# Operand sums, attention order, weight casts and a statistic's ring moved in a transformer layer on one core

## The chip, the core and the metric

The kernel runs on one core of a Trainium2 chip. The core has five engines that run side by side, each with its own in-order list of instructions: TensorE (PE) multiplies matrices, VectorE (DVE), ScalarE (ACT) and GpSimd (POOL) work element by element, SyncE (SP) does nothing here but start transfers. Transfers between DRAM and the on-chip memory run on 16 DMA engines; the instruction that starts one stands in an engine's list like any other, and waits there until its destination is free and its source is written. The metric is the device time of one execution in microseconds; the median of several runs counts.

## The reference

One step of one layer of a decoder, on 2048 new prompt tokens and 32 sample tokens (8 sequences of 4), model width 1024, all in fp32:

```
h = rmsnorm(x, n1);  z = h @ w_in            # split: hq hf hi hg | sq sk sv | ga gb
y_a = (rmsnorm(hgrn(hq, hf, hi, state)) * silu(hg)) @ w_up_a     # recurrent branch, 4 heads of 128
y_b = sink_attention(rotary(sq), rotary(sk), sv, window 128) @ w_up_b   # 8 query heads, 2 key heads of 64
m = sigmoid(ga) * y_a + sigmoid(gb) * y_b
x = x + m @ w_o
x = x + square(relu(rmsnorm(x, n2) @ w_ff1)) @ w_ff2             # width 4096
y = rmsnorm(x, normf)
```

The sample tokens attend to a cache of 128 keys and values for each sequence and start from a given recurrent state. Besides y, the kernel returns the new keys, values and states.

## The kernel before, in words

**Arithmetic.** Each fp32 operand is split in two parts: ScalarE casts it to a high half (fp32r), VectorE subtracts to get the low half. A product is three matmuls: high by high, high by low, low by high. The helpers are `split_out` (L257-259) for a source elsewhere and `split_in` (L143) in place. Large products with a whole pair of blocks use one level of a Strassen scheme (seven products for eight): `strassen_T` (L375-397) runs over pairs of weight columns (`Wpair`, L272-310) and chunks of tokens (`Unit`); its operands are A11, A12, A22 and the sums S1 to S4. `Wpair.early` loads and casts the two weight blocks B11 and B21 with which a pair's first two products (the tiles fB and fC) begin; `early` runs for the first pairs before the main loop, `rest` and `late` make the others.

**Stages.** The tokens are cut into four blocks of 512 (the fourth also holds the 32 sample tokens), in two pairs. For each block follow the projections by parts of w_in (C_HI values of the recurrence, C_HQ, C_SQ queries, C_SQ + 512 keys and values, C_HF), the attention, the levels of the recurrence, gate B (loop L1269-1283, eight steps j), gate A (L1290-1306, eight steps) and the output projection with w_o (L1384-1405, eight columns in four pairs). Before the third block a Strassen stage, named z, computes HQ, GA and GB for the whole second pair (L824-880). Its operands come from hidden values kept in DRAM; in front of it stand the projections skv and sq for the third and fourth block, whose results go to DRAM (zqk) from staging tiles (L826-837). After the fourth block follow, for each pair, the two feed-forward stages f1 (`strassen_T` again) and f2.

**The operand sums.** The first pair's feed-forward needs S1 to S4 of its normalised values h2d, which lie in DRAM. For each of four row groups k, `fr_load(k)` (L898-903) takes three tiles of the ring t4 and issues four loads on SP; `fr_sums` (L905-907) does four additions on VectorE (L605-608) and issues four stores dS on POOL's queue (L610). The ring t4 has three tiles, so one set fills it, and the next load waits until the stores of the one before have landed. The attention takes its cache tiles (kc, vc and others) from the same ring. Loads (L583) and additions are pinned. Before the change, sets 0 and 1 are in the C_HI projection of the third block (`fr_hook`, L922-930), sets 2 and 3 in the C_SQ and keys-and-values projections of the fourth (`sq_fr`, L914-917).

**What sets the order.** The program is traced in the order in which it is written; a planner then orders each engine's instructions by priority and by its own estimate of when each is ready. `pin` (L139-140) holds an instruction behind the one traced just before it on the same engine. TensorE's order in the attention and the recurrence is written out by hand: a list at L1131 of turns (T_), scores (S_), probabilities (P_) and values (V_) for the four subtiles, with `fill` steps between them that are matmuls of the C_HF projection. Small jobs are hung into loops: `late_at` (L559-568) calls the next of a list (for each block: the statistic `n2.stat`, its spreading `n2.spread` over the partitions, and `h2_out`, which scales and stores the normalised values) at given places of a projection; the list `todo` gives one job to each of the eight columns of the output projection (L1322-1383). In the third block the jobs are `reload` of the next block's operand on SP and `recast`, its split, both pinned; in the fourth they are loads and casts of the feed-forward's operands. In the fourth block's C_HI the sample tokens' scores, transposes (`smp_turn`) and values are hung in by `smp_at` (L1040). PSUM tiles come from four rings, mm, tp, hg and sw; the statistic of the last block (L1412) uses hg, as do the fC tiles of the feed-forward.

Weight tiles come from a ring of 12; a unit takes three (as loaded, high half, low half).

Of the kernel before, what the change touches and what calls it, by code (L numbers as in the profile page):

```python
# [16 lines left out]
P = 128  # L17
# [4 lines left out]
NKV = 2  # L22
# [21 lines left out]
def tile_hybrid_step(  # L44
# [225 lines left out]
    class Wpair:  # L270
# [2 lines left out]
        def __init__(u, N, n, src, wt):  # L273
            u.N, u.n, u.src, u.wt, u.ops = f"{N}_{n}", n, src, wt, {}

        def done(u, name, raw):
            v = (u.wt if name in ("T3", "T4") else wtile)(F32R, f"w1{name}_{u.N}").rearrange("p (s k c) -> p s k c", s=2, k=4)
            split_out(v[:, 0], v[:, 1], raw)
            u.ops[name] = v

        def early(u):
            v = wtile(F32, f"w1r0_{u.N}").rearrange("p (s k c) -> p s k c", s=2, k=4)
            for kh in range(2):
                nc.sync.dma_start(v[:, kh], u.src(u.n, kh)[:, 0:P].rearrange("(k p) c -> p k c", p=P))
                u.done(f"B{kh + 1}1", v[:, kh])

        def rest(u):
            b = []
# [86 lines left out]
    def strassen_T(N, npairs, src, chunks, A, st, fin, ahead, early, mid, free, wt):  # L375
        ws = [Wpair(N, n, src, wt) for n in range(npairs)]
        nch = len(chunks)
        units = [Unit(i, ws[i // nch], *chunks[i % nch], A, st, fin) for i in range(npairs * nch)]
        if free:
            units[-1].free, units[-1].ring = True, mm_ps  # L380
        for i in range(ahead):
            if i % nch == 0:
                units[i].pair.early()
            units[i].a(i < 4)
            early(i, units[i])
        for i, u in enumerate(units):
# [49 lines left out]
    def kmaj(x, r0, nk, c0, n):  # L436
        return x[r0 * P:(r0 + nk) * P, c0:c0 + n].rearrange("(k p) t -> p k t", p=P)
# [144 lines left out]
        for x, (r0, c0) in zip(r, ((0, 0), (4, 0), (0, Th), (4, Th))):  # L582
            pin(nc.sync.dma_start(x, h2d[b][(r0 + k) * P:(r0 + k + 1) * P, c0:c0 + Th]))  # L583

    def ff_sums(b, v, r, k, loaded=False):
# [19 lines left out]
        pin(tt(s1, a21, a22, ALU.add), loaded)  # L605
        pin(tt(s2, s1, a11, ALU.subtract), loaded)
        pin(tt(a21, a11, a21, ALU.subtract), loaded)
        pin(tt(a12, a12, s2, ALU.subtract), loaded)
        for n, x in (("S2", s2), ("S1", s1), ("S3", a21), ("S4", a12)):
            nc.gpsimd.dma_start(sd[b][n][k * P:(k + 1) * P, :], x)  # L610

    def op_load(b, v, x, r0, c0, now=True):
        out = []
# [18 lines left out]
    for bi in range(nblk):  # L632
# [193 lines left out]
        if zs and not odd:  # L826
            stage = [wk.tile([P, 768], F32, tag="stg", bufs=4, name=f"stg{c}") for c in range(ncb)]

            def st_skv(ps, kind, c, nr):
                nc.scalar.copy(stage[c][:, 512:768], ps)  # L830

            def st_sq(ps, kind, c, nr):
                nc.scalar.activation(qk_out(stage[c][:, 0:512]), qk_in(ps), AF.Copy, scale=HD ** -0.5)
                nc.scalar.dma_start(zqk[sb][c * P:(c + 1) * P, :], stage[c])
# [70 lines left out]
        def fr_sums():  # L905
            k, r = fr.pop()
            ff_sums(0, None, r, k, True)

        if not zs:
            colN512(C_HI, f"hi{B}", ev_v, *((late_at(0, 2, 3), None) if bi else (first_stat, first_split)))  # L910
# [1 line left out]
                first = bi == 0 and h < 2  # L912
                colT(C_HQ, h, f"hq{B}{h}", ev_q, sw_ps if first else mm_ps, (lambda: spread(rb0, rs0[:, 0], bt, "first")) if first and h == 0 else None)
        if odd or not zs:  # L914
            sq_late = late_at(0, 2, 3)
            sq_fr = iter([lambda: fr_load(2), none, none, lambda: [fr_sums(), fr_load(3)], none, none, none, fr_sums, none] if zs else [none] * 9)
            colN512(C_SQ, f"sq{B}", ev_sq, lambda i, ul: [sq_late(), next(sq_fr)()])
            colN(C_SQ + 512, f"skv{B}", ev_skv, lambda: next(sq_fr)())
        else:
            for c in range(ncb):  # L920
                nc.gpsimd.dma_start(qkv[:, c, :], zqk[sb][c * P:(c + 1) * P, :])
            nc.gpsimd.dma_start(qW, kmaj(zd[sb], 0, HH, z0 + ns, bt))  # L922
            def fr_hook(i, ul):
                if i == 0:
                    fr_load(0)
                elif i == 2:
                    fr_sums()
                    fr_load(1)
                elif i == 3:
                    fr_sums()  # L930

            colN512(C_HI, f"hi{B}", ev_v, fr_hook)
# [104 lines left out]

        if zs and odd:
            nc.gpsimd.dma_start(qW, kmaj(zd[sb], 0, HH, z0 + ns, bt))
            smp_at = {0: lambda: [smp_scores(kv) for kv in range(NKV)], 1: lambda: [smp_turn(kv) for kv in range(NKV)], 2: smp_values} if smp else {}  # L1040
            colN512(C_HI, f"hi{B}", ev_v, lambda i, ul: smp_at[i]() if i in smp_at else None)

        kts = {-1: k_last}
# [84 lines left out]
                    n -= 1  # L1128

        T_, S_, P_, V_ = swa_turn, swa_scores, swa_probs, swa_values  # L1130
        for f, c in ((T_, 0), (fill, 6), (S_, 0), (T_, 1), (fill, 12), (S_, 1), (T_, 2), (fill, 30), (P_, 0), (fill, 10), (V_, 0), (S_, 2), (T_, 3), (fill, 10), (P_, 1),  # L1131
                     (fill, 10), (V_, 1), (S_, 3), (fill, 10), (P_, 2), (fill, 8), (V_, 2), (fill, 16), (P_, 3), (fill, 8), (V_, 3)):
            f(c * len(segs) if f is fill else c)
        fill(1000)
# [135 lines left out]
        for j in range(KD):  # L1270
            if j % 2 == 0:
                ub = unit(
                    [(kv * HD, (kv + 1) * HD, w_ub[kv * 256:(kv + 1) * 256, j * P:j * P + 256].rearrange("(k p) c -> p k c", p=HD)) for kv in range(NKV)],
                    4, f"ub{B}{j}")
            for _ in gate(C_GB, j, ub, b_acts, lambda j, t0, n: pb[:, j, t0:t0 + n], "b"):
                pass
            if zs and j < 4:
                nc.vector.tensor_copy(ga[:, 2 * j, 0:1], pb[:, j, 0:1])
                nc.gpsimd.dma_start(ga[:, 2 * j:2 * j + 2, :], kmaj(zd[sb], HH + KD + 2 * j, 2, z0, T))
            if sb == 0 and j % 2 == 1:  # L1280
                sum_next()
            elif sb == 0:
                side_next(bi)
# [7 lines left out]
        for j in range(KD):  # L1291
            if sb == 0 and j % 2 == 1:
                sum_next()
            elif sb == 0:
                side_next(bi)
            if j == 0 and zs:
                ua_next = unit_rows(w_ua, 0, 4, 0, 256, f"ua{B}0", True)
            if j % 2 == 0 and zs:
                ua = ua_next
                if j + 2 < KD:  # L1300
                    ua_next = unit_rows(w_ua, 0, 4, (j + 2) * P, 256, f"ua{B}{j + 2}", True)
            elif j % 2 == 0:
                ua = unit_rows(w_ua, 0, 4, j * P, 256, f"ua{B}{j}")
            for t0, n, o in gate(C_GA, j, ua, a_acts, lambda j, t0, n: ga[:, j, t0:t0 + n] if zs else t2(f"ta_{B}{j}_{t0}")[:, 0:n], "a"):
                (nc.vector if j >= KD - 2 else nc.gpsimd).tensor_tensor(o, o, pb[:, j, t0:t0 + n], ALU.add)
                split_out(mT[j // 4][:, 0, j % 4, t0:t0 + n], mT[j // 4][:, 1, j % 4, t0:t0 + n], o)

        while side.get(bi):
            side_next(bi)
# [38 lines left out]
        elif not odd:  # L1348
# [405 lines left out]
```

## Time and profile before

| | us |
|---|---|
| median of 3 runs | 2844.31 (2840.08 to 2846.9) |
| the profiled execution | 2856.07 |
| its span | 2854.1 |
| TensorE busy | 2743.9 (96%) |
| VectorE busy | 1788.6 (63%) |
| ScalarE busy | 1110.6 (39%) |
| GpSimd busy | 489.8 (17%) |

All durations in the text are from the profiled execution, whose mean granted TensorE clock was 0.987 of full speed. Its time has been read thus: an engine's busy time is the sum of its instructions; a wait is the time in which an engine stood before an instruction, put down to what ended it; the chain of waits is the way back from the last instruction through whatever released each step.

### The profile page before, as it was taken

The page shows a single profiled execution, that of the slowest core. Times are in us where ns is not written, and L with a number is a line of the kernel's source. Part 1 is how long each engine was busy: PE and PEld are TensorE (multiplying, and loading weights), DVE is VectorE, ACT ScalarE, POOL GpSimd, SP SyncE. Part 2 cuts the span into 40 slices and gives each one's busy share as a digit, 9 for nine tenths or more (in the row PEclk, how much of TensorE's full clock was granted, in tenths as well). Part 3 has the DMA queues.
Part 4 walks back from the last instruction along what each step waited for, and adds up shares of the span by engine and source line. Part 5 has one row for each costly group of instructions (what it writes and reads, how often), then busy time and mean ns, then how long its engine had stood idle before and what let it go on. Part 6 is the DMA issues. An engine that isn't in the chain of part 4 may idle for free.

```text
span 2854.1 us, 50092 instructions
## 1 busy us (share of the span) xinstructions
PE 2743.9 (96%) x20053; PEld 2414.4 (85%) x20053; DVE 1788.6 (63%) x2905; ACT 1110.6 (39%) x2070; POOL 489.8 (17%) x782
## 2 busy tenths in 40 slices
PE   8999999999899989989899999999998999999998
PEld 7778877788799967767898888887888999999997
DVE  5675646646764375535667777765567777664556
ACT  4542445323344353324325333434443233343332
POOL 1100211002200101320231222220002333320001
PEclk9999999999999999999999999999999999999999
DMA  5237662377733533651266444696566444485553
GB/s 187 76 107 236 206 190 67 105 235 264 231 122 113 158 91 106 211 169 51 87 196 208 161 162 159 228 320 230 195 195 205 157 144 152 146 288 187 188 187 114
DMA packets 344481, 487.60 MB, mean 171 GB/s; under 512 B 23432, under 2 KB 220824, under 8 KB 344248
## 3 DMA queue, kind: packets, MB, share of 16 engines
q1 hardware_dynamic: 289112, 329.10, 37.0%
q0 software_dynamic: 42880, 140.22, 13.6%
q10 hardware_dynamic: 12256, 15.08, 1.5%
q8 instruction: 157, 2.57, 0.4%
q14 instruction: 76, 0.62, 0.1%
HBM read 353.64 MB, written 130.68 MB: 170 GB/s over the span
## 4 chain that ended last, share of the span: by engine, by line
PE 76%; DMA 8%; DVE 5%; issue 5%; ACT 3%; POOL 2%; SPq 0%; POOLq 0%; ACTq 0%; DVEq 0%
PE f L1585 6%; PE f L1584 6%; PE f L1586 6%; PE fB_f L264 4%; PE fB_f L266 4%; PE fB_f L265 4%; PE fD_f L264 2%; PE fD_f L266 2%; PE fD_f L265 2%; PE wob L1394 1%; PE wob L1392 1%; PE wob L1393 1%; PE fB_z L264 1%; PE fB_z L266 1%; PE fB_z L265 1%
## 5 line engine op out<-in xcount | busy, mean ns | idle before, releaser
L1584 PE MATMUL f<-f2S,hw2T 128*128 128x264 f32 (+1 forms) x576 | 184.5, 320 | 2.5 <-ACT hw2T L151 2.5
L1586 PE MATMUL f<-f2S,lw2T 128*128 128x264 f32 (+1 forms) x576 | 184.2, 320 | 1.0 <-DVE lw2T L152 1.0
L1585 PE MATMUL f<-f2S,hw2T 128*128 128x264 f32 (+1 forms) x576 | 184.1, 320 | 0.0
L264 PE MATMUL fB_f<-S,w1T_f 128*128 128x264 f32 (+1 forms) x384 | 123.0, 321 | 3.1 <-ACT c_f L327 2.5
L1584 PE MATMUL f<-f2A,h_w2B 128*128 128x264 f32 (+1 forms) x384 | 122.4, 319 | 0.0
L1585 PE MATMUL f<-f2A,h_w2B 128*128 128x264 f32 (+1 forms) x384 | 122.3, 319 | 0.0
L1586 PE MATMUL f<-f2A,l_w2B 128*128 128x264 f32 (+1 forms) x384 | 122.3, 318 | 0.0
L265 PE MATMUL fB_f<-S,w1T_f 128*128 128x264 f32 (+1 forms) x384 | 122.2, 319 | 0.0
L266 PE MATMUL fB_f<-S,w1T_f 128*128 128x264 f32 (+1 forms) x384 | 121.9, 319 | 0.0
L152 DVE TENSOR_TENSOR lw2T<-lw2T,hw2T 128x1024 fp32r<-128x1024 f32 x64 | 78.2, 1224 | 65.9 <-ACT hw2T L151 65.0
L1584 PEld LDWEIGHTS f<-f2S,hw2T 128*128 128x128 f32 x576 | 108.7, 189 | 10.5 <-ACT hw2T L151 3.0
L151 ACT CAST hw2T<-lw2T 128x1024 fp32r<-128x1024 f32 x64 | 67.2, 1051 | 128.8 <-DMA lw2T<-w_T 128.8
L1586 PEld LDWEIGHTS f<-f2S,lw2T 128*128 128x128 f32 x576 | 108.4, 188 | 9.5 <-DVE lw2T L152 1.8
L1585 PEld LDWEIGHTS f<-f2S,hw2T 128*128 128x128 f32 x576 | 108.8, 189 | 7.5
L1394 PE MATMUL wob<-m_b,l_wob 128*128 128x512 f32 (+2 forms) x320 | 112.1, 350 | 2.8 <-DVE l_wob L258 2.8
L1392 PE MATMUL wob<-m_b,h_wob 128*128 128x512 f32 (+2 forms) x320 | 112.1, 350 | 0.0
L1393 PE MATMUL wob<-m_b,h_wob 128*128 128x512 f32 (+2 forms) x320 | 111.8, 349 | 0.0
L152 DVE TENSOR_TENSOR f2S<-f2S 128x1024 fp32r<-128x1024 f32 (+1 forms) x64 | 79.0, 1240 | 43.8 <-ACT f2S L151 43.2
L258 DVE TENSOR_TENSOR w1T_f<-w1r_f,w1T_f 128x512 fp32r<-128x512 f32 x128 | 87.4, 688 | 26.2 <-ACT w1T_f L257 25.9
L257 ACT CAST w1T_f<-w1r_f 128x512 fp32r<-128x512 f32 x128 | 77.1, 619 | 65.2 <-PE fB_f L266 27.9
L1511 POOL DMA_DIRECT2D u_A<-c_f x106 | 57.3, 541 | 239.2 <-DVE c_f L1495 230.9
L258 DVE TENSOR_TENSOR l_w2B<-rw2B,h_w2B 128x1024 fp32r<-128x1024 f32 x48 | 58.8, 1224 | 62.6 <-ACT h_w2B L257 52.7
(845 smaller groups left out, 9302.8 us busy)
## 6 DMA issues: line engine op xcount, KB each, us to landing
w1r_f<-w_ff SPq DMA_DIRECT2D x64, 512.0 KB
lw2T<-w_T SPq DMA_DIRECT2D x64, 512.0 KB
rw2B<-w_ff SPq DMA_DIRECT2D x48, 512.0 KB
f2S<-u_S SPq DMA_DIRECT2D x32, 528.0 KB
ws<-w_ff SPq DMA_DIRECT2D x32, 512.0 KB
r_wob<-w_o SPq DMA_DIRECT2D x32, 512.0 KB
f2S<-u_S SPq DMA_DIRECT2D x32, 512.0 KB
u_S<-s_f POOLq DMA_DIRECT2D x96, 132.0 KB, 2.3
```

The costliest lines, as they stand in the source:

```text
L152: pin(nc.vector.tensor_tensor(lo, F(lo), F(hi), ALU.subtract), on)
L257: pin(nc.scalar.copy(dh, src), on)
L258: pin(nc.vector.tensor_tensor(dl, src, F(dh), ALU.subtract), on)
L264: nc.tensor.matmul(ps, wh, ah, start=(first and k == 0), stop=False, skip_group_check=not first)
L265: nc.tensor.matmul(ps, wh, al, start=False, stop=False, skip_group_check=not first)
L266: nc.tensor.matmul(ps, wl, ah, start=False, stop=(last and k == 3), skip_group_check=not first)
L1392: nc.tensor.matmul(p, wh, ah, start=(k == 0), stop=False)
L1393: nc.tensor.matmul(p, wh, al, start=False, stop=False)
L1394: nc.tensor.matmul(p, wl, ah, start=False, stop=(k == KD - 1))
L1584: nc.tensor.matmul(ps, wh, ah, start=first, stop=False, skip_group_check=cont)
L1585: nc.tensor.matmul(ps, wh, al, start=False, stop=False, skip_group_check=cont)
L1586: nc.tensor.matmul(ps, wl, ah, start=False, stop=lastk, skip_group_check=cont)
```

## The change

1. `early` gets a flag that pins its casts and subtractions; `strassen_T` sets it for the first pair, in z and in both feed-forward stages:

```diff
-                units[i].pair.early()
+                units[i].pair.early(i == 0)
```

2. In front of z, the queries come before the keys and values. The store of zqk goes with the later one, and the second block's late jobs move:

```diff
-            colN(C_SQ + 512, f"skv{B}", st_skv, late_at(1))
-            colN512(C_SQ, f"sq{B}", st_sq, late_at(0, 1))
+            colN512(C_SQ, f"sq{B}", st_sq, late_at(0, 2))
+            colN(C_SQ + 512, f"skv{B}", st_skv, late_at(1))
```

3. The operand sums leave the projections of the third and fourth block. Sets 0 and 1 go into the third block's gates, sets 2 and 3 into its output projection, whose other jobs move by up to a column (`fr_sums` and `ff_sums` also get a queue as an argument, which stays POOL's everywhere):

```diff
+        fr_at = {("b", 0): lambda: fr_load(0), ("b", 5): fr_sums, ("b", 6): lambda: fr_load(1), ("a", 3): fr_sums} if zs and not odd else {}
...
-            todo += [lambda: [reload(0, 0), reload(0, 2)], none, lambda: recast(0, 0), lambda: [recast(0, 2), reload(1, 0)], lambda: reload(1, 2), lambda: recast(1, 0), lambda: recast(1, 2)]
+            todo += [lambda: [fr_load(2), reload(0, 0)], lambda: reload(0, 2), fr_sums, lambda: [fr_load(3), recast(0, 0)],
+                     lambda: [recast(0, 2), reload(1, 0)], lambda: [fr_sums(), reload(1, 2)], lambda: recast(1, 0), lambda: recast(1, 2)]
```

4. In the fourth block's C_HI the sample's transposes and values come one unit later:

```diff
-            smp_at = {0: lambda: [smp_scores(kv) for kv in range(NKV)], 1: lambda: [smp_turn(kv) for kv in range(NKV)], 2: smp_values} if smp else {}
+            smp_at = {0: lambda: [smp_scores(kv) for kv in range(NKV)], 2: lambda: [smp_turn(kv) for kv in range(NKV)], 3: smp_values} if smp else {}
```

5. In the attention of every block six matmuls of fill move from in front of P_0 to behind it:

```diff
-(T_, 2), (fill, 30), (P_, 0), (fill, 10), (V_, 0)
+(T_, 2), (fill, 24), (P_, 0), (fill, 16), (V_, 0)
```

6. The last block's statistic takes its PSUM tiles from another ring:

```diff
-            n2.ring = hg_ps
+            n2.ring = sw_ps
```

More of the change, by code (lines that the diff above doesn't have):

```diff
@@ L274, in __init__, with done, early @@
             u.N, u.n, u.src, u.wt, u.ops = f"{N}_{n}", n, src, wt, {}
-        def done(u, name, raw):
+        def done(u, name, raw, on=False):
             v = (u.wt if name in ("T3", "T4") else wtile)(F32R, f"w1{name}_{u.N}").rearrange("p (s k c) -> p s k c", s=2, k=4)
-            split_out(v[:, 0], v[:, 1], raw)
+            split_out(v[:, 0], v[:, 1], raw, on)
             u.ops[name] = v
-        def early(u):
+        def early(u, on=False):
             v = wtile(F32, f"w1r0_{u.N}").rearrange("p (s k c) -> p s k c", s=2, k=4)
@@ L284, in early @@
                 nc.sync.dma_start(v[:, kh], u.src(u.n, kh)[:, 0:P].rearrange("(k p) c -> p k c", p=P))
-                u.done(f"B{kh + 1}1", v[:, kh])
+                u.done(f"B{kh + 1}1", v[:, kh], on)
         def rest(u):
@@ L583, in ff_rows, with ff_sums @@
             pin(nc.sync.dma_start(x, h2d[b][(r0 + k) * P:(r0 + k + 1) * P, c0:c0 + Th]))
-    def ff_sums(b, v, r, k, loaded=False):
+    def ff_sums(b, v, r, k, loaded=False, q=nc.gpsimd):
         Th = Ths[b]
@@ L609, in ff_sums @@
         for n, x in (("S2", s2), ("S1", s1), ("S3", a21), ("S4", a12)):
-            nc.gpsimd.dma_start(sd[b][n][k * P:(k + 1) * P, :], x)
+            q.dma_start(sd[b][n][k * P:(k + 1) * P, :], x)
     def op_load(b, v, x, r0, c0, now=True):
@@ L830, in st_skv @@
                 nc.scalar.copy(stage[c][:, 512:768], ps)
+                nc.scalar.dma_start(zqk[sb][c * P:(c + 1) * P, :], stage[c])
             def st_sq(ps, kind, c, nr):
                 nc.scalar.activation(qk_out(stage[c][:, 0:512]), qk_in(ps), AF.Copy, scale=HD ** -0.5)
-                nc.scalar.dma_start(zqk[sb][c * P:(c + 1) * P, :], stage[c])
+            colN512(C_SQ, f"sq{B}", st_sq, late_at(0, 2))
             colN(C_SQ + 512, f"skv{B}", st_skv, late_at(1))
-            colN512(C_SQ, f"sq{B}", st_sq, late_at(0, 1))
             Th = Ths[sb]
@@ L903, in fr_load, with fr_sums @@
             ff_rows(0, fr[-1][1], k)
-        def fr_sums():
+        def fr_sums(q=nc.gpsimd):
             k, r = fr.pop()
-            ff_sums(0, None, r, k, True)
+            ff_sums(0, None, r, k, True, q)
+        fr_at = {("b", 0): lambda: fr_load(0), ("b", 5): fr_sums, ("b", 6): lambda: fr_load(1), ("a", 3): fr_sums} if zs and not odd else {}
         if not zs:
@@ L914, in tile_hybrid_step @@
         if odd or not zs:
[L915 to L918, printed above, removed]
+            colN512(C_SQ, f"sq{B}", ev_sq, late_at(0, 2, 3))
+            colN(C_SQ + 512, f"skv{B}", ev_skv)
         else:
@@ L922, in tile_hybrid_step @@
             nc.gpsimd.dma_start(qW, kmaj(zd[sb], 0, HH, z0 + ns, bt))
[L923 to L932, printed above, removed]
+            colN512(C_HI, f"hi{B}", ev_v)
         ob = op(6, F32R, "ob_" + B)[:, 0:8 * T].rearrange("p (s k t) -> p s k t", s=2, k=4)
@@ L1130, in tile_hybrid_step @@
         T_, S_, P_, V_ = swa_turn, swa_scores, swa_probs, swa_values
-        for f, c in ((T_, 0), (fill, 6), (S_, 0), (T_, 1), (fill, 12), (S_, 1), (T_, 2), (fill, 30), (P_, 0), (fill, 10), (V_, 0), (S_, 2), (T_, 3), (fill, 10), (P_, 1),
+        for f, c in ((T_, 0), (fill, 6), (S_, 0), (T_, 1), (fill, 12), (S_, 1), (T_, 2), (fill, 24), (P_, 0), (fill, 16), (V_, 0), (S_, 2), (T_, 3), (fill, 10), (P_, 1),
                      (fill, 10), (V_, 1), (S_, 3), (fill, 10), (P_, 2), (fill, 8), (V_, 2), (fill, 16), (P_, 3), (fill, 8), (V_, 3)):
@@ L1279, in tile_hybrid_step @@
                 nc.gpsimd.dma_start(ga[:, 2 * j:2 * j + 2, :], kmaj(zd[sb], HH + KD + 2 * j, 2, z0, T))
+            if ("b", j) in fr_at:
+                fr_at["b", j]()
             if sb == 0 and j % 2 == 1:
@@ L1306, in tile_hybrid_step @@
                 split_out(mT[j // 4][:, 0, j % 4, t0:t0 + n], mT[j // 4][:, 1, j % 4, t0:t0 + n], o)
+            if ("a", j) in fr_at:
+                fr_at["a", j]()
         while side.get(bi):
```

## The prediction

> **What bounds the kernel now.** I read the page first, then TensorE's waits, then the chain of waits at the longest of them, and last the timelines of the engines on which the change puts work.
>
> ```profile
> span 2854.1 us, 50092 instructions
> PE 2743.9 (96%) x20053; PEld 2414.4 (85%) x20053; DVE 1788.6 (63%) x2905; ACT 1110.6 (39%) x2070; POOL 489.8 (17%) x782
> ```
>
> TensorE is busy for 2743.9 of 2854.1 us, so it sets the time, and 110.2 us of idle time are all that a change of order can touch. The change takes no matmul away and adds none. So the working is a list of TensorE's waits: columns are the waiting tile and line, who released it, microseconds in total, times, longest.
>
> ```profile
> PE sp_b2c L1070 <- ACT kt_b2c L953: 9.2, 1, 9.2
> PE kcT L973 <- DMA kc<-cache_swa_k: 8.0, 1, 8.0
> PE fB_f L264 <- DVE y L1591: 4.6, 1, 4.6
> PE pTs L1019 <- DVE ss L1014: 4.0, 1, 4.0
> PE fB_z L264 <- ACT stg L833: 2.8, 1, 2.8
> PE fC_z L264 <- DVE p_z L342: 2.6, 1, 2.6
> PE n_fb L216 <- DVE p_f L342: 2.1, 1, 2.1
> PE po_b1c L1117 <- DVE sm_b1c L1090: 1.7, 1, 1.7
> PE po_b0c L1117 <- DVE pc_b0c L1108: 1.2, 1, 1.2
> ```
>
> The first, second and fourth rows are 21.2 us in the third and fourth block, and the change touches each. Now what stands behind the first, in rows of SP's timeline and of the chain of waits (start, duration, what):
>
> ```profile
> 988.28 1.85 SPq L583 DMA_DIRECT2D fr<-h2d  x4
> 990.23 1.08 SPq L138 DMA_DIRECT2D r_hfb<-w_in  x2
> 997.30 2.81 DMA dS<-fr
> 1000.26 1.80 SPq L583 DMA_DIRECT2D fr<-h2d  x4
> 1002.16 7.14 DMA r_hgb<-w_in
> 1009.37 1.04 ACT h_hgb L257
> 1012.10 3.62 PE sp_b2c L1070 x32
> 1019.20 1.99 PE sp_b2c L1070 x32
> ```
>
> SP's queue had issued a weight load by 991.31 and then stood until 1000.26 in front of the second set of fr loads, whose tiles come free only when the sums of the first set have landed in DRAM (997.30 + 2.81). The weight load r_hgb stood behind, ScalarE's cast h_hgb waited for that, and the casts of the attention's keys wait behind the cast. After the wait the first 32 score matmuls took 3.62 us, the next 32 only 1.99: TensorE's clock was low after idling.
>
> **The change part by part.** All is summed against the profiled execution (2856.07 us with its 2854.1 us span). It lies 11.8 us above the median of the runs, 2844.31, and I carry the difference over to the median unchanged.
>
> *The third block's attention start.* The fr loads and sums leave this block's C_HI, so r_hgb could go out at 991.3 instead of 1002.16, which is 10.9 us earlier and more than the wait of 9.2. With the wait go 3.62 - 1.99 = 1.6 us of slow matmuls. Next late are the keys' own casts on ScalarE; I leave 2 us for them: **-8.8** (bounds -5 and -10.8).
>
> *The fourth block's cache turn, and the sample's scores.*
>
> ```profile
> 1250.72 2.87 DMA dS<-fr
> 1253.71 4.15 DMA kc<-cache_swa_k
> 1259.93 0.43 PE ps_hib_-1_11965 L191
> 1268.77 9.69 DMA r_hfb<-w_in
> 1278.54 1.04 ACT h_hfb L257
> 1282.63 0.45 PE pTs L1019
> 1283.29 0.43 PE ps_hib_-1_11965 L191
> 1288.73 0.23 PE ps_hib L192
> ```
>
> kc lies in the same ring of three tiles as fr: its load starts at 1253.71, just after the last sums landed (1253.59). After the change the last sums belong to the third block's output projection, which ends before the fourth block begins, so the 8.0 us go, and about three matmuls at 0.43 instead of 0.23: **-8.6** (-6.5 and -8.7). The sample's transposes pTs waited 4.0 us for a softmax whose ScalarE steps stood behind the cast h_hfb (1278.54), which waited for its load. One place later they have one more unit of C_HI in front, 24 matmuls of 0.23, which is 5.5 us and more than 4.0. From 1283.29 to 1288.7 about twelve matmuls cost 0.43 instead of 0.23, another 2.4: together **-6** (-4 and -6.4).
>
> *The order of the attention.* V_0 gets 16 matmuls of fill in front instead of 10, P_0 gets 24 instead of 30. Six at 0.23 are 1.4 us, taken off the waits of po on the two rows shown: 1.4 of the 1.7 and all of the 1.2, and a little of smaller waits of the same kind. **-3** (-4 to +1, since P_0 now comes 1.4 us earlier and may wait for its softmax).
>
> *The statistic in the sw ring.* n_fb waited 2.1 us for DVE to read a feed-forward tile in the hg ring. In the sw ring, which the first feed-forward units don't use, that wait goes: **-2** (0 to -2.1).
>
> *The pinned casts.* This is the part with a price. A pinned cast stands behind whatever was traced before it on its engine, and at the start of the feed-forward that is the cast of S1.
>
> ```profile
> 1518.65 1.13 ACT L257 CAST w1B_f<-w1r_f 128x512 fp32r<-128x512 f32 x2
> 1534.82 0.69 DVE L258 TENSOR_TENSOR w1B_f<-w1r_f,w1B_f 128x512 fp32r<-128x512 f32 x1 [0.20 <-ACT w1B_f L257]
> 1535.51 0.40 PE L264 MATMUL fB_f<-A,w1B_f 128*128 128x512 f32 x1
> 1536.80 1.98 ACT L151 CAST S<-S 128x1024 fp32r<-128x1024 f32 x2
> 1537.86 2.36 DVE L152 TENSOR_TENSOR S<-S 128x1024 fp32r<-128x1024 f32 x2 [0.21 <-ACT S L151]
> ```
>
> Before, pair 0's weights were cast at 1518.65, and the first matmul ran at 1535.51. S1's casts end at 1538.78 and its subtractions at 1540.22. One weight cast (0.57) behind the former gives a first matmul at about 1539.4; the low half (0.69) gives the third at 1540.9 instead of 1536.0: 4.9 us, and 2.4 for the slow matmuls after such a pause (as at 1283.29), 7.3 in all. The other bound is 0: TensorE's order is not pinned here, the later pairs' weights are not pinned either, and two groups of 12 matmuls (5.5 us) of the next pair could fill the hole. No row decides between them; I take the middle, **+4** (0 to +7.3). [...]
>
> The same pin in the stage before the third block stands behind the casts of its operands, with the projections sq and skv exchanged and the late steps of the second block moved; the stores of zqk, as many as before, go out on ScalarE's queue with skv, now the later of the two. Its start waits 2.8 + 2.6 us now; the exchange can take that away (-5) or the pinned casts can add as much as at the feed-forward (+6): **0**. In the second feed-forward the start waits 4.6 us for y already, and two casts of 1.13 us together fit under that: **0** (up to +3).
>
> *The sums in their new places.* Each set is four DVE instructions and four issues on POOL.
>
> ```profile
> L605 DVE TENSOR_TENSOR fr<-fr x4: 685/692/695, 995.6 to 1249.0; 128x512 f32<-128x512 f32 x4
> L610 POOL DMA_DIRECT2D dS<-fr x16: 540/540/586, 996.6 to 1251.9; - x16
> 1156.20 1.22 DVE L258 TENSOR_TENSOR l_uab<-r_uab,h_uab 128x1024 fp32r<-128x1024 f32 x1
> PE yab L167 <- DVE l_uab L258: 0.8, 1, 0.8
> 1142.33 1.28 POOL L1305 TENSOR_TENSOR ga_b<-ga_b,pb_b 128x512 f32<-128x512 f32 x1 [1.07 <-DVE ga_b L1267]
> 1148.76 2.20 POOL L1305 TENSOR_TENSOR ga_b<-ga_b,pb_b 128x512 f32<-128x512 f32 x1 [2.06 <-DVE ga_b L1267]
> ```
>
> 4 x 0.69 = 2.8 us of DVE. In gate A's third step they are traced just ahead of l_uab, a pinned instruction for which TensorE already waits 0.8: nearly all of it shows, **+2.5** (0 to +6, the upper end if the waiting DMAs' issues, 4 x 0.54 = 2.2, hold up POOL's additions too). In gate B and in the output projection DVE has room between evictions; the only reader near is the low half of w_o: **+0.7** for the two sets there (0 to +3), 0 for the set in gate B. POOL's addition takes 1.28 us in one row and 2.20 in another of the same shape. [...]
>
> Sum: -8.8 - 8.6 - 6 - 3 - 2 + 4 + 0 + 2.5 + 0.7 = -21.2. That gives 2834.9 for an execution like the profiled one, and 2844.31 - 21.2 = **2823** for the median.
>
> **The rivals.**
>
> *Half the gain (0.15).* ScalarE works in order, and the casts of the keys and of the sample's softmax stand behind weight casts whichever load is late. If that keeps 4.8 us of the first wait and all 6 of the sample's, the sum is -10.4: 2834. For it: both waits end on ScalarE behind a cast. Against it: in both chains the load, not the cast, is the long piece (7.14 and 9.69 against 1.04).
>
> *More (0.13).* The hole at the feed-forward is filled by the next pair (-4), and the exchange of sq and skv clears the 5 us at the stage's start: -30, which is 2814.
>
> *No change (0.10).* The fr loads were not what held SP: r_hgb might have no free weight tile either until about 1002, and kc might be held by another tile of the ring. Then the first two terms (17.4) fall out and -3.8 is left: 2840.5, within 0.2% (5.7 us, about what a measurement of this kernel can tell from no change). Against it: the loads follow each other on SP without a pause at 1000.26 to 1002.16, and dS landed 0.1 us before kc started.
>
> *Slower (0.08).* The moved fr loads stay pinned on SP and wait in turn for the sums before them.
>
> ```profile
> 1169.76 0.97 SPq L138 DMA_DIRECT2D r_wob<-w_o  x2
> 1162.00:1206.00 44.00, 43.95 (x195) 36.06 (x194) 27.72 (x28) 19.76 (x24) 14.31 (x16) 1.00 0.57 186
> ```
>
> In gate B's seventh step and in steps 0 and 3 of the projection, weight loads stand behind them. Each could cost what it cost before, 9.2 + 1.6 = 10.8; three are 32.4, and the sum becomes +11: 2855. It decides where SP stands longer than the weights' lead. The projection takes 44 us for eight columns, so the weights of the third pair, issued at 1169.8, are wanted at 1162 + 22 = 1184: 14 us, of which 7 for landing and 2.3 for cast and subtraction are used. SP would have to stand over 5 us; it stood 9.0 in the third block's attention, but there the loads came right behind the sums. Here one or two steps lie between.
>
> **How the numbers follow.** My forecast has the chance 0.54; the likeliest time is 2823. Three cases are faster by over 0.2% (below 2838.6): 0.54 + 0.15 + 0.13 = 0.82. Within it lies no change, 0.10; above 2850.0 the last, 0.08. The range starts at 2812, which holds the better rival and little beyond it, and ends at 2840, which holds the half gain and leaves out most of the case of no change and the slower one: about 0.17 lie above and 0.03 below.
>
> **What would show it.** In the changed profile the waits of sp_b2c on kt_b2c, of kcT on kc and of pTs on ss should be gone or under 2 us, and the score matmuls of the third block should all take 2.0 per 32. fB_f should show a first wait of 4 to 5 us at the first feed-forward's start, or another pair's group in its place. l_uab in the third block should have TensorE waiting some 3 us. Wrong would be a wait of over 5 us on a weight cast in the third block's gates or projection, or a wait of over 8 us still at the attention's start.

## The result and the profile after

The changed kernel takes 2818.86 us (median, 2811.82 to 2820.34) where the kernel before takes 2842.20 on the same chip: a ratio of 0.9911 with a 95% interval of 0.9889 to 0.9933, so 23.3 us less, and clear of the 0.2% that can be told apart. The forecast was 21.2 us less, a median of 2823.

The profiled execution of the changed kernel took 2811.82 us and is the shortest of its runs; that of the kernel before (2856.07) lay above its median. The two profiles are thus 44 us apart, 21 more than the medians, and stages that the change doesn't touch differ by 2 us and more. So stages are compared here over all profiles, and a difference counts only where it stays whenever the part in question stays.

The first lines of the page after:

```profile
span 2810.0 us, 50089 instructions
PE 2730.1 (97%) x20053; PEld 2403.9 (86%) x20053; DVE 1791.2 (64%) x2905; ACT 1110.0 (40%) x2070; POOL 490.9 (17%) x782
```

The same number of matmuls, and 13.8 us less TensorE busy time: the mean granted clock rose from 0.987 to 0.993, so most of this should be matmuls that ran at a low clock before. A change of order thus touched more than the idle time of 110.2 us that the prediction began from. The waits of TensorE after, those that answer to the rows shown of before and those that are new (waiting tile and line, releaser, us in total, times, longest):

```profile
PE yab L167 <- DVE l_uab L258: 3.8, 1, 3.8
PE wob L1388 <- ACT h_wob L257: 3.2, 2, 1.7
PE n_fb L216 <- DVE carry L245: 2.0, 1, 2.0
PE fB_f L264 <- DVE y L1587: 1.7, 1, 1.7
PE ps_skvb L176 <- ACT stg L830: 1.5, 1, 1.5
PE fB_f L264 <- ACT w1B_f L257: 0.6, 1, 0.6
PE kcT L964 <- ACT SV_b L940: 0.3, 1, 0.3
PE po_b0c L1108 <- DVE pc_b0c L1099: 0.3, 1, 0.3
```

The 9.2 of the attention's start, the 8.0 of the cache, the 4.0 of the sample and the 2.1 of the statistic in its old form are gone; kcT waits 0.3. In their place stand 3.8 us in gate A, 3.2 on w_o's weights, and some 2.6 at the feed-forward's start.

The lengths of the stages, each from the first matmul of one tile to the first of the next, worked out from the starts in the traces (us):

| stage | before | after | sums_old | fill_old | turn_old | sq_old | no_pin | pin_z | ring_hg | sums_c |
|---|---|---|---|---|---|---|---|---|---|---|
| second block, attention | 42.2 | 38.8 | 38.8 | 42.2 | 38.8 | 38.8 | 38.8 | 38.8 | 38.8 | 38.8 |
| second block's output projection to the end of z | 295.2 | 288.7 | 289.0 | 288.3 | 288.4 | 292.5 | 294.6 | 290.6 | 289.4 | 288.8 |
| third block, attention to gate B | 98.4 | 85.9 | 99.2 | 91.1 | 82.7 | 85.6 | 86.7 | 87.9 | 86.2 | 83.9 |
| third block, gate A | 23.9 | 29.1 | 24.0 | 29.6 | 29.6 | 29.5 | 29.1 | 28.3 | 29.6 | 23.9 |
| third block, output projection | 43.9 | 50.2 | 43.8 | 49.5 | 49.6 | 50.4 | 50.3 | 49.6 | 49.4 | 46.3 |
| fourth block, queries | 28.7 | 30.4 | 28.7 | 29.8 | 30.5 | 29.6 | 30.1 | 29.8 | 29.8 | 28.7 |
| keys and values, cache turn | 24.4 | 15.9 | 23.9 | 15.9 | 15.9 | 15.9 | 15.9 | 15.9 | 15.9 | 15.9 |
| C_HI with the sample | 44.7 | 35.6 | 37.2 | 35.6 | 41.0 | 35.8 | 35.6 | 35.6 | 35.6 | 35.6 |
| last output projection to first fB_f | 48.4 | 52.2 | 52.2 | 52.2 | 52.2 | 52.2 | 48.4 | 48.4 | 48.4 | 48.4 |

From before to after the rows change by -3.4, -6.5, -12.5, +5.2, +6.3, +1.7, -8.5, -9.1 and +3.8: -23.0 in all, close to the 23.3 of the medians; the statistic's ring acts outside these rows. Since the two profiles are 44 us apart, a single row is worth what the other columns confirm.

### The profile page after: what moved, and what is told of

It is laid out like the page before. It is cut to its first block, busy times and chain, and to the rows that moved or that the text cites. A ratio compares the mean times of both kernels' runs of the same rounds, so it can differ in the third digit from the quotient of the medians.

```text
span 2810.0 us, 50089 instructions
## 1 busy us (share of the span) xinstructions
PE 2730.1 (97%) x20053; PEld 2403.9 (86%) x20053; DVE 1791.2 (64%) x2905; ACT 1110.0 (40%) x2070; POOL 490.9 (17%) x782
## 3 DMA queue, kind: packets, MB, share of 16 engines
q0 software_dynamic: 42880, 140.22, 13.8%
## 4 chain that ended last, share of the span: by engine, by line
PE 78%; DMA 6%; DVE 6%; issue 5%; ACT 2%; POOL 2%; SPq 0%; POOLq 0%; DVEq 0%; ACTq 0%
PE f L1581 6%; PE f L1582 6%; PE f L1580 6%; PE fB_f L264 4%; PE fB_f L266 3%; PE fB_f L265 3%; PE fD_f L264 2%; PE fD_f L266 2%; PE fD_f L265 2%; PE ps_hfb L684 2%; PE fB_z L264 1%; PE fB_z L266 1%; PE fB_z L265 1%; PE wob L1390 1%; PE gab L166 1%
## 5 line engine op out<-in xcount | busy, mean ns | idle before, releaser
L1507 POOL DMA_DIRECT2D u_S<-s_f x144 | 77.7, 541 | 109.0 <-DVE s_f L1502 92.4
```

Of the source, the lines that this page charges most:

```text
L1507: nc.gpsimd.dma_start(us[o][u.n // 4][u.n % 4 * P:(u.n % 4 + 1) * P, u.t0:u.t0 + u.ln], y_)
```

## The experiments

Each kernel is the changed one with the edit shown; the time before is that of the kernel before on the same chip, and the ratio is to it. A ratio's interval reaches 4 to 6 us to each side, so where two kernels are closer than that, the stages and waits carry the argument and not the times.

**Sums at their old places (sums_old).**

```diff
-        fr_at = {("b", 0): lambda: fr_load(0), ("b", 5): fr_sums, ("b", 6): lambda: fr_load(1), ("a", 3): fr_sums} if zs and not odd else {}
+        fr_at = {}
...
+            colN512(C_HI, f"hi{B}", ev_v, fr_hook)
```

(`fr_hook`, `sq_fr` and `todo` are those of the kernel before)

> The changed kernel with the operand sums alone put back where they were (third block's C_HI, fourth block's queries and keys). My theory: the old places caused the attention's wait of 9.2 us with 1.6 us of slow matmuls, and the cache's wait of 8.0 with 0.7, together 19.5; the new places cost 5.2 in gate A, 6.4 in the output projection and 1.7 in the projection after it, together 13.2 by the two profiles. So this kernel is 6 us slower than the changed one, about 2825, with waits of 9 us on kt_b2c and 8 us on kc back. Rival: other edits (the exchange of queries and keys, the order of the attention) removed those waits; then they stay away and the time falls by 13 to about 2806.

Measured: 2828.56 us against 2846.60, ratio 0.9936 (0.9922 to 0.9951). Against the changed kernel's 0.9911 that is 7 us worse, with intervals that overlap; 6 were expected. Its waits and, at the attention's start, its chain of waits:

```profile
PE sp_b2c L1072 <- ACT kt_b2c L955: 8.3, 1, 8.3
PE kcT L975 <- DMA kc<-cache_swa_k: 7.5, 1, 7.5
```

```profile
988.14 2.73 DMA dS<-fr
993.00 6.09 DMA r_hgb<-w_in
999.16 1.04 ACT h_hgb L257
1001.66 0.18 ACT kt_b2c L955
```

Both old waits are back, with the same steps, and gate A, the projection and the queries have their old lengths to 0.1 us. So the move of the sums removes 13.3 + 8.0 us and 1.6 in C_HI (behind the cache's wait; in the kernel before, matmuls there start 0.43 us apart), and costs 5.1 + 6.4 + 1.7: 10 us net in the stages, 7 by the ratio. The other 18 us of this kernel's gain over before come from the other edits.

**The same, loads on POOL's queue (old_pool).**

```diff
-            pin(nc.sync.dma_start(x, h2d[b]...
+            pin(nc.gpsimd.dma_start(x, h2d[b]...
```

> The kernel of the run sums_old (the sums at their old places, all else as changed) with the fr loads issued on POOL's queue instead of SP's. The attention's wait came back with the old places (8.3 us); this run asks whether it is SP's standing or the sums themselves. My theory: SP stood in front of the second set's loads with r_hgb behind; with the loads on POOL the wait on kt_b2c goes and the third block's attention (first kT_b2c to first ybb) takes 86 to 88 us instead of 99.2, while the cache's wait of 7.5 us, which is about the tiles, stays. Rival: the weight load r_hgb has no free tile before, or the sums' work on VectorE and POOL delays the keys; then about 99 us stay.

Measured: 2824.91 us against 2847.19, ratio 0.9922 (0.9905 to 0.9938).

```profile
PE kcT L975 <- DMA kc<-cache_swa_k: 8.1, 1, 8.1
PE sp_b2c L1072 <- ACT kt_b2c L955: 2.5, 2, 1.6
```

```profile
997.39 0.69 DVE L605 TENSOR_TENSOR fr<-fr 128x512 f32<-128x512 f32 x1 [5.04 <-DMA fr<-h2d]
999.92 1.22 DVE L258 TENSOR_TENSOR l_hgb<-r_hgb,h_hgb 128x1024 fp32r<-128x1024 f32 x1
1001.17 1.05 ACT L257 CAST h_hgb<-r_hgb 128x1024 fp32r<-128x1024 f32 x1 [6.12 <-DVE l_hgb L258]
```

The cache's wait stays, as expected of a wait for tiles. Of the attention's 8.3 us 2.5 are left, in two pieces, and its stage takes 92.8, between the two theories: SP's standing was 5.8 us of the wait and about half of the stage's 13.3 (6.4). The rows lead to the larger piece of what is left (1.6 us), and it is the rival's way: VectorE stood 5.0 us in front of the pinned sums until their loads landed, the subtraction l_hgb came behind them, and ScalarE's next cast, which waited 6.1 us for that, stands in front of the keys' cast.

**All sums in gate B (sums_b).**

```diff
-        fr_at = {("b", 0): lambda: fr_load(0), ("b", 5): fr_sums, ("b", 6): lambda: fr_load(1), ("a", 3): fr_sums} if zs and not odd else {}
+        fr_at = {("b", 0): lambda: fr_load(2 * odd), ("b", 3): fr_sums, ("b", 4): lambda: fr_load(2 * odd + 1), ("b", 7): fr_sums} if zs else {}
```

(todo of the output projection as before the change)

> The changed kernel with all four sets of sums in gate B: sets 0 and 1 in the third block's, sets 2 and 3 in the fourth's (load at step 0, sums at step 3, load at step 4, sums at step 7); the output projection's list as before the change. My theory: gate A and the projection lengthened by 5.2 and 6.4 us because the sums lie in a chain of VectorE, GpSimd and ScalarE there, and the loads in front of w_o's weights; gate B has VectorE idle some 2 us per step. Then 13 us go: about 2806, with the yab wait on l_uab at 0.8 and no wait on h_wob. Rival: a set costs its 2.8 us wherever VectorE and GpSimd evict; then gate B grows by 5 in each block and the time is about 2816.

Measured: 2816.27 us against 2846.60, ratio 0.9894 (0.9877 to 0.9911). The projection and the queries are back at 43.5 and 28.7 us, but gate A takes 28.3 in the third block and 28.2 instead of 24.2 in the fourth. The time is the rival's, but not by the rival's way: gate B did not grow (39.1 us in the third block, as before). The second set's loads landed only after gate A had begun, so its sums stood there after all. The cache load had moved up on SP and waited there for their stores, a load of gate A's weights stood behind it, and TensorE waited for that one's cast:

```profile
PE yab L165 <- ACT h_uab L257: 3.1, 1, 3.1
```

**Earlier in gate B (sums_b2), casts pinned in z alone.**

```diff
+        fr_at = {("b", 0): lambda: fr_load(2 * odd), ("b", 1): lambda: [fr_sums(), fr_load(2 * odd + 1)], ("b", 6): fr_sums} if zs else {}
...
-                units[i].pair.early(i == 0)
+                units[i].pair.early(i == 0 and N[0] == "z")
```

> Casts pinned in z alone, and all sums in gate B, earlier than in the first try: load at step 0, sums and the next load at step 1, sums at step 6, in the third and fourth block. In the first try the second set's loads landed only after gate A had begun, and its sums and stores then stood in gate A's chain and behind them a weight load on SP (waits of 3.1 us on h_uab). My theory: with the sums done before gate A it takes 24 us in both blocks instead of 28.3 and 28.2, and with the 3.8 us of the feed-forward's start the time is about 2804 where the changed kernel has 2819. Rival: the stores dS and the cache load that then moves up on SP still delay the weights of gate A: 28 us stay in one block or both, about 2812.

Measured: 2827.01 us against 2847.86, ratio 0.9926 (0.9907 to 0.9944): a miss, the rival's way and worse. Gate A takes 36.5 us in the third block and 28.2 in the fourth. SP's timeline in the third (start, duration, issues):

```profile
1106.45 2.25 SPq L583 DMA_DIRECT2D fr<-h2d  x4
1108.82 1.15 SPq L138 DMA_DIRECT2D r_uab<-w_up_a  x2
1123.81 0.37 SPq L957 DMA_DIRECT2D kc<-cache_swa_k  x1
1131.55 0.34 SPq L958 DMA_DIRECT2D out_new_k_sample<-kc  x1
1131.99 4.71 SPq L138 DMA_DIRECT2D r_uab<-w_up_a  x1
```

The fourth block's cache load and its copy to the output now stand in front of gate A's weights, presumably because the planner saw the t4 tiles free early; the copy waits for the load, and gate A's weights r_uab stood behind it until 1131.99. So an edit that frees a resource early can let something else move in.

**Tiles held until the projection (sums_c), casts pinned in z alone.**

```diff
+        fr_at = {("b", -1): lambda: fr_load(0), ("b", 0): lambda: [fr_sums(), fr_load(1)], ("b", 6): fr_sums, ("a", 4): lambda: fr_load(2)} if zs and not odd else {}
+        if zs and odd:
+            fr_at = {("b", 0): lambda: fr_load(3), ("b", 3): fr_sums}
...
+            todo += [..., lambda: reload(1, 2), lambda: [recast(1, 0), fr_sums()], lambda: recast(1, 2)]
```

> Casts pinned in z alone; set 0 is loaded ahead of gate B and summed at its step 0, set 1 loaded there and summed at step 6, set 2 loaded at gate A's step 4 and summed at the sixth column of the output projection, set 3 loaded and summed at steps 0 and 3 of the fourth block's gate B. The second try left a load landing at gate A's start and freed the tiles so early that the cache's load and its copy to the output moved up on SP, ahead of gate A's weights (SP stood from 1123.8 to 1132.0). My theory: with the tiles held until the projection and the second set there in time, gate A takes 24 us, the projection 44 and the next projection 29 in the third block, gate A 24 in the fourth, so 13 + 3.8 us less than the changed kernel: about 2802, a ratio of 0.986 to the kernel before. Rival: each set costs its 2.8 us of VectorE wherever it lies; then about 2810.

Measured: 2807.81 us against 2845.01, ratio 0.9865 (0.9845 to 0.9885). This is the fastest kernel here: its interval lies below the changed kernel's and below that of pin_z (next), from which it differs by the places of the sums and of the jobs beside them; against that it is 10 us faster by the ratios. Its time lies between the two numbers expected, so the stages must decide. Gate A is back at 23.9 and 24.2 us and the queries at 28.7. The projection takes 46.3 where 44 were expected, with two waits of under 1 us at its start and slow matmuls behind them (granted clock 0.84 from 1137 to 1142), and the third block's gate B 40.1 instead of 39.1.

```profile
PE wob L1393 <- DVE l_wob L258: 3.6, 3, 1.6
PE wob L1391 <- ACT h_wob L257: 0.8, 1, 0.8
PE yab L167 <- DVE l_uab L258: 0.6, 1, 0.6
```

The wait of 3.8 on l_uab is 0.6 here, and two sets cost 1.0 us in gate B. So a set doesn't cost its 2.8 us wherever it lies.

**Casts pinned in z alone (pin_z), and none pinned (no_pin).**

```diff
-                units[i].pair.early(i == 0)
+                units[i].pair.early(i == 0 and N[0] == "z")
```

(that is pin_z; no_pin has `early()`)

> The changed kernel with the first pair's casts pinned in the z stage alone, not in the two feed-forward stages. My theory: the pin delays the first feed-forward's start by 3.8 us (projection's start to first fB_f 52.2 us against 48.4); without it about 2815. Rival: the statistic's own wait of 2.0 us on the carry, which now stands ahead of fB_f, sets that start; then the time is within 1 us of the changed kernel, about 2819.

> The changed kernel with no cast pinned at all. My theory: the pin is what took away the z stage's two waits at its start (2.8 and 2.6 us); without it they return and the feed-forward gains 3.8, so about 2820. Rival: the exchange of queries and keys took them away; then they stay away, and the time is that of the kernel pinned in z alone, about 2815.

Measured: pin_z 2818.22 us against 2846.60, ratio 0.9902 (0.9886 to 0.9917); no_pin 2823.97, ratio 0.9913 (0.9895 to 0.9930). The feed-forward's start is 48.4 us in both and in every kernel without the pin there, 52.2 in every kernel with it: 3.8 us. This projection and z together take 290.6 us with the pin and 294.6 without, so the pin in z is worth 4, or 6 against the 288.7 of the changed kernel, which has the same code there as pin_z. By the medians pin_z is 6 us faster than no_pin, by the ratios 3. Its own number came out as the rival's: it is 0.6 us faster than the changed kernel by the medians and 2.6 by the ratios, so the 3.8 us are shown by the stage, not by the time. In no_pin neither theory holds: the two waits at z's start do not return as they were, but the wait on a staging tile (ps_skvb) is 2.8 us instead of 1.5.

**Queries and keys in the old order (sq_old).**

```diff
+            colN(C_SQ + 512, f"skv{B}", st_skv, late_at(1))
+            colN512(C_SQ, f"sq{B}", st_sq, late_at(0, 1))
```

(and the store of zqk back in `st_sq`)

> The changed kernel with queries and keys in front of z in the old order and the second block's late steps at their old places; the casts stay pinned. My theory: the pin and the exchange each take part of the waits at z's start; with the pin alone one of the two waits (2.6 us) stays away and the other (2.8) returns: about 2822. Rival: the pinned casts stand behind the operand's casts, which wait longer in the old order, and the start costs 6 us more than before: 2828.

Measured: 2827.99 us against 2847.86, ratio 0.9933 (0.9913 to 0.9953).

```profile
PE fB_z L264 <- ACT stg L833: 1.9, 1, 1.9
PE fC_z L264 <- DVE p_z L342: 1.9, 1, 1.9
```

Both waits at z's start are back where one was expected, each somewhat shorter than the 2.8 and 2.6 of before, and the stage is 3.8 us longer. The time is near the rival's 2828, but the rival's way, a start slower than before, is not there (292.5 against 295.2). So pin and exchange each do little without the other: 295.2 with neither, 294.6 and 292.5 with one, 288.7 with both. The exchange leaves a wait of 1.5 on a staging tile (ps_skvb, above) as its price.

**The sample's places back (turn_old).**

```diff
-... 2: lambda: [smp_turn(kv) for kv in range(NKV)], 3: smp_values}
+... 1: lambda: [smp_turn(kv) for kv in range(NKV)], 2: smp_values}
```

> The changed kernel with the sample's transposes and values alone back at their earlier places in the fourth block's C_HI. My theory: the place itself is too early for the softmax, so the wait of pTs returns with slow matmuls behind it: from the first kcT to the first kT_b3c about 43 us instead of 36.5, and the time is 7 us longer, about 2826. Rival: the softmax was late only because the weight load r_hfb was late, which the fr loads on SP had delayed; with those gone the transposes wait for nothing and the time stays at 2819.

Measured: 2830.84 us against 2847.86, ratio 0.9934 (0.9913 to 0.9955).

```profile
PE pTs L1010 <- DVE mxs L996: 2.3, 1, 2.3
PE pTs L1010 <- DVE ss L1005: 1.3, 1, 1.3
```

3.6 us of waits are back with no fr load near; C_HI takes 41.0 us instead of 35.6, where the kernel before had 44.7. So the place is worth 5.4 us. The kernel before has about the same wait (4.0) and 3.7 us more in the stage, and these are slow matmuls: its matmuls start 0.43 us apart in three stretches (from 1259.9, 1283.3 and 1295.4). The rival is refuted: with no fr load near, the softmax still stands behind the cast h_hfb, whose load lands at 1252.05.

**The old fill (fill_old).**

```diff
-(T_, 2), (fill, 24), (P_, 0), (fill, 16), (V_, 0)
+(T_, 2), (fill, 30), (P_, 0), (fill, 10), (V_, 0)
```

> The changed kernel with the old fill in the attention (30 in front of P_0, 10 behind). My theory: the waits of po return, 2.3 us in the second block with about 1 us of slow matmuls, 1 us each in the first, third and fourth: 5 us longer, about 2824. Rival: only the second block's wait is real (1.7 us) and the others are noise: 2821.

Measured: 2832.38 us against 2847.86, ratio 0.9945 (0.9926 to 0.9965), by the ratios 10 us worse than the changed kernel, with intervals that overlap.

```profile
PE po_b2c L1108 <- DVE sm_b2c L1081: 2.1, 1, 2.1
PE po_b1c L1108 <- DVE sm_b1c L1081: 1.7, 1, 1.7
PE po_b3c L1108 <- DVE pc_b3c L1099: 1.2, 3, 0.5
PE po_b0c L1108 <- DVE pc_b0c L1099: 1.2, 1, 1.2
```

All waits of po add up to 7.8 us here, to 0.8 in the changed kernel and to 5.3 in the kernel before. The third block's first one is 2.1 us here and was 0.6 there: there the first scores ran slowly behind the wait of 9.2 (3.62 us for 32, then 1.99), and ScalarE had copied them 2.7 us before the next scores began (1016.40 and 1019.13); here it is 1.2 us (996.60 and 997.84), behind a weight cast that had been done before the scores there. So the long wait had hidden part of this one. Stages: 3.4 us in the second block and 5.2 in the third; the latter stretch varies from 82.7 to 87.9 among kernels whose code in it is the same, so of the 5.2 only the waits are sure. The fill is worth 7 us by the waits.

**The statistic's ring back (ring_hg), casts pinned in z alone.**

```diff
-            n2.ring = sw_ps
+            n2.ring = hg_ps
```

> Casts pinned in z alone, as in the run pin_z, and the last block's statistic back in the hg ring. My theory: the ring is what removed the wait of 2.1 us on p_f; it returns and the stretch from the first fB_f to the first f is 2 us longer than with the sw ring (308.8), the time 2 us longer than pin_z's. Rival: the wait comes from the order of TensorE, not the ring, and nothing changes.

Measured: 2823.19 us against 2845.01, ratio 0.9921 (0.9903 to 0.9938), about 5 us worse than pin_z by the ratios, whose intervals overlap.

```profile
PE n_fb L216 <- DVE p_f L342: 2.1, 1, 2.1
```

The wait of 2.1 on p_f is back and the stretch from the first fB_f to the first f is 312.3 us instead of 308.8 in pin_z. The ring's share is thus 2 to 3.5 us.

## Why the prediction was right, point by point

The time came out 2 us from the forecast for the change, and the main mechanism holds: fr loads pinned on SP, waiting for the sums before them, held the attention's weights, and their tiles the cache. That the number fits so well is luck: by the rows of the table the attention with its fill, z and the sample gained 13.7 us more than forecast, gate A, the projection and the queries cost 10.0 more, and these cancelled. Of the signs named, the three waits are gone, l_uab shows 3.8, and no wait in the gates or the projection is over 5 us; the score matmuls take 2.0 per 32. The sign for the feed-forward's start did not come (below).

- **Attention's start, -8.8.** Right in kind, too small: 13.3 in the stage by sums_old, which is the wait, the slow matmuls behind it (17 scores in 2.28 us) and the variation of that stretch. That SP's standing was the way is shown for about half of it; a part went through VectorE, which stood in front of the sums (old_pool).
- **Cache, -8.6.** Measured -8.5, and back to within half a microsecond in sums_old.
- **Sample, -6.** Right in kind, too small: -9.1, of which 5.4 are the place (turn_old). I counted the wait and the slow matmuls right behind it, and missed a second slow stretch of 3.4 us, at 1295.4, in front of which TensorE had not waited.
- **Fill, -3.** Too small: 7 us by the waits and 10 by the ratio, 3.4 in the second block's attention alone. I took it from two rows of before and left the smaller ones (5.3 us in all) nearly out, and the third block's wait was partly hidden by a longer one. When a wait is removed, the next late thing has to be priced with it, and there it was this one: 2.1 us instead of 0.6.
- **Ring, -2.** 2 to 3.5 (ring_hg).
- **Pinned casts at the feed-forward, +4.** Measured +3.8, but in neither of the ways whose middle I took, so the fit is luck. TensorE showed no first wait of 4 to 5 us and did not take the next pair's matmuls; it took the last block's statistic, which had stood behind the first units before.

```profile
1501.99 1.14 ACT L257 CAST w1B_f<-w1r_f 128x512 fp32r<-128x512 f32 x2
1501.02 1.06 PE L216 MATMUL n_fb<-ident,carry 128*68 128x128 f32 x8 [2.02 <-DVE carry L245]
1502.66 0.50 PE L264 MATMUL fB_f<-A,w1B_f 128*128 128x512 f32 x1 [0.58 <-ACT w1B_f L257]
```

The casts do stand behind S1's, as forecast, and fB_f waits 0.6 on them after n_fb's 2.0 on the carry. No slow matmuls follow (granted clock 1.00 from 1501 to 1506).

- **Second feed-forward, 0 (up to +3).** Its wait for y is 1.7 us (4.6 before), but 0.6 to 4.6 over the kernels here: no cost of the pin shows.
- **z, 0 (-5 to +6).** Measured -6.5, outside the gain that I had allowed. I took the exchange and the pin for alternatives; they need each other.
- **Gate A, +2.5 (0 to +6).** Measured +5.2. VectorE there, after the change:

```profile
1128.92 0.69 DVE L605 TENSOR_TENSOR fr<-fr 128x512 f32<-128x512 f32 x1
1130.12 0.69 DVE L606 TENSOR_TENSOR fr<-fr,fr 128x512 f32<-128x512 f32 x1
1130.73 1.75 DVE L607 TENSOR_TENSOR fr<-fr,fr 128x512 f32<-128x512 f32 x1
1132.40 0.68 DVE L608 TENSOR_TENSOR fr<-fr,fr 128x512 f32<-128x512 f32 x1
1133.01 1.21 DVE L258 TENSOR_TENSOR l_uab<-r_uab,h_uab 128x1024 fp32r<-128x1024 f32 x1
1130.50 1.43 POOL L1298 TENSOR_TENSOR ga_b<-ga_b,pb_b 128x512 f32<-128x512 f32 x1
```

The sums stand in front of l_uab, as forecast; one of them took 1.75 us instead of 0.69 while POOL added. The wait grew from 0.8 to 3.8 us, about the price that I had given; the rest of the 5.2 are slow matmuls behind it (granted clock 0.50 from 1134.27 to 1138.6), which I had not priced.

- **Output projection, +0.7 (0 to +3).** The step that failed: +6.3, and 1.7 more in the queries after it. SP after the change, at the projection's start and middle, and what it waited for in the whole run (total, times, longest):

```profile
1134.36 1.91 SPq L583 DMA_DIRECT2D fr<-h2d  x4
1137.36 9.79 SPq L138 DMA_DIRECT2D r_wob<-w_o  x4
1169.31 2.24 SPq L583 DMA_DIRECT2D fr<-h2d  x4
1171.65 0.93 SPq L138 DMA_DIRECT2D r_wob<-w_o  x2
SPq L583 <- DMA dS<-fr: 47.2, 4, 20.9
SPq L957 <- DMA dS<-fr: 12.7, 1, 12.7
```

and ScalarE where the two waits on h_wob (3.2 us together) end:

```profile
1152.36 0.63 ACT L241 ACTIVATE carry<-x_b 128x512 f32<-128x512 f32 x1 [6.86 <-DVE x_b L1394]
1152.90 1.03 ACT L257 CAST h_wob<-r_wob 128x1024 fp32r<-128x1024 f32 x1
1177.29 1.04 ACT L257 CAST h_wob<-r_wob 128x1024 fp32r<-128x1024 f32 x1 [2.76 <-DMA r_wob<-w_o]
```

The term priced VectorE's work; SP was left to the rival "slower". SP stood 20.9 us in front of the second of these loads, until the stores of the sums before them had landed, and the last pair's two weights of w_o went out behind it. The second wait on h_wob ends with the landing of one of them, and behind it the matmuls start 0.43 us apart until 1183.4, some 1.8 us more. At the first wait no load was missing: the packets of the four weights issued from 1137.36 end at 1149.97, but ScalarE stood idle until a column's square at 1152.36, with the cast behind it; before the change that cast stood ahead of the square. Why the order changed is not shown. In the queries the same thing happens once more: the cache load waits 12.7 us on SP for the last sums' stores, and the weights of the queries stand behind it.

So it is that rival in small. I had let it begin where SP stands for over 5 us against the weights' lead; SP stood four times as long, but four of the six weights that stood behind fr loads had gone out ahead of the long stand. Its mechanism acted, at a quarter of its price at most (8.0 of 32.4 us).

## What to carry to other kernels

A transfer that waited for its tile held every later one in its queue here, for up to 20.9 us; ask of each pinned load what stands behind it, both where it is taken from and where it is put. When a wait of 9 us is removed, price what comes next: here part of a softmax's delay had been hidden by it (2.1 us instead of 0.6). And a resource freed early can be taken early: keeping the tiles busy (sums_c) was better here than freeing them (sums_b2).

## What the runs showed of the hardware

The clock. After the wait of 3.8 us in gate A the matmuls start 0.43 us apart, later 0.23; three windows of the changed kernel (the granted clock is the third number from the end):

```profile
1129.00:1141.00 12.00, 7.94 (x24) 6.05 (x25) 8.47 (x13) 2.55 (x5) 4.87 (x6) 0.72 0.62 198
1154.00:1178.00 24.00, 22.66 (x96) 17.77 (x96) 14.28 (x13) 7.88 (x10) 10.33 (x11) 1.00 0.51 174
1178.00:1192.00 14.00, 13.57 (x51) 10.43 (x52) 9.54 (x10) 4.74 (x7) 7.12 (x10) 0.88 0.69 245
```

The window with the wait of 3.8 shows 0.72. Two shorter waits of about the same length came out differently: behind the one of 1.7 us, which ends at 1153.98, the clock is 1.00; behind the one of 1.5, which ends at 1178.39, it is 0.88, and the matmuls start 0.43 us apart from 1179.98 to 1183.4. In the kernel before they did so from 1295.4 to 1298.8 with no wait ahead, right behind 36 narrow matmuls of the sample's values (clock 0.57 from 1295 to 1299). The length of a wait alone does not tell here whether it costs the clock.

Additions on VectorE and GpSimd at the same time. The sum of 1.75 us began 0.23 after POOL's addition and ended 0.55 after it; in the projection two others that began during an addition on POOL took 1.78 us (L606, from 1164.71) and 1.77 us (L607, from 1181.44) and ended 0.54 and 0.55 after it. The other 13 sums on fr of the changed kernel and the 16 of the kernel before, none of which began during one, took 0.68 to 0.70 us. What held the three is not shown. In gate A this cost 1.06 us (1.75 - 0.69) of the 5.2, and some 2 us are slow matmuls.
